# The odd feed-forward block's plain products moved from the end into the first pair of a Strassen-tiled encoder block

## The chip, the cores and the metric

The kernel runs on one core of a Trainium2 chip. The metric is device time in microseconds (us), the median of the runs shown. A core has five engines, each with its own instruction queue that is worked off in order: TensorE (PE, matrix products), VectorE (DVE), ScalarE (ACT), GpSimd (POOL) and SyncE (SP, which here only issues DMAs). Semaphores order them against one another.

## The reference

One layer of a streaming encoder on 256 positions of 2048 channels, in float32: RMS norm, a combined input projection, a gated spatial branch, a sparse-attention branch, an output projection, a residual add; then the part that matters here, a norm and a SwiGLU feed-forward block with 5632 hidden columns, a residual add, and a last norm:

```python
        hn = rms_norm(h, norm2_g[l])
        h = h + (jax.nn.silu(hn @ w_ff_gate[l]) * (hn @ w_ff_up[l])) @ w_ff_down[l]
    return rms_norm(h, final_g)
```

## The kernel before

Every product is made to float32 accuracy from two rounded halves: an operand is split into a high part (ACT, line 74) and the rest (DVE, line 75), and `mm3` (lines 89 to 91) issues three matmuls, high x high, high x low of the weights, low x high. All weights pass through these two splits, so each weight tile costs a load on SP's queue, an ACT copy and a DVE subtraction before PE can use it.

The feed-forward block has 11 column blocks of 512, numbered 0 to 10. Blocks 0 to 9 are done in five pairs, block 10 is the odd one. For a pair, `s_group` makes a gate or an up product over all 16 tiles of the contraction, in eight chunks of 1 MB. Four of them (j = 0 to 3) go by Strassen's scheme: seven products in place of eight, 21 matmuls, but DVE first makes four sums of weight tiles (lines 534 to 536) and both the raw tiles and the sums are split. The other four (j = 4 to 7) are plain: 24 matmuls and one split of 128x2048. The chunks come in the order 0, 4, 1, 5, 2, 3, 6, 7, so Strassen chunks 2 and 3 stand next to each other. `plain_group` is the ordinary product, with chunks of 24 matmuls and one split each; it makes block 10's gate and up products and every down product (`down_one`).

Buffers: 3 for raw weights, 3 each for split halves of 128x2048 (plain chunks and split sums share them), 2 each for those of 128x1536, one for sums. PSUM has four banks "aux" and four "acc"; an `s_group` uses all eight.

Order: PE's order is that of the code, since lines 625 and 626 fix it by hand. Those of ACT, DVE and SP are set by a scheduler at build time, by priorities in code order. The code order before is: pair 0's gate and up groups; pairs 1 to 4, each with gate, two down products of the pair before it, up, the other two; block 10's gate, the transposes of blocks 8 and 9 (`a_operand`, on PE, then split by ACT and DVE), block 10's up; the down products of blocks 8 and 9 (two chunks for each of the four output columns n), among them block 10's down weights are split and kept; at the end the closing section (`last`) multiplies block 10 with the kept weights, adds the residual and makes the last norm, one half of the rows after the other.

Of the kernel before, what the change touches and what calls it, by code (L numbers as in the profile page):

```python
# [12 lines left out]
AF = mybir.ActivationFunctionType  # L13
ALU = mybir.AluOpType
# [5 lines left out]
KT = D // P  # L20
# [9 lines left out]
NFB = FF // 512  # L30
# [10 lines left out]
def block_kernel(ctx: ExitStack, tc: tile.TileContext, a, out):  # L41
# [5 lines left out]
    nc = tc.nc  # L47
# [10 lines left out]
    def t_tile(name, dt=F32R):  # L58
        return tp.tile([P, 4, T], dt, tag="T", name=name)
# [28 lines left out]
    def mm3(o, lh, ll, rh, rl, start, stop, **kw):  # L88
        nc.tensor.matmul(o, lh, rh, start=start, stop=False, **kw)  # L89
        nc.tensor.matmul(o, lh, rl, start=False, stop=False, **kw)  # L90
        nc.tensor.matmul(o, ll, rh, start=False, stop=stop, **kw)  # L91

    def nat_group(w, ks, x, name):


        acc = [acc_tile(f"{name}_{t}") for t in range(2)]
        for c in range(len(ks) // 2):
            wh, wl = wchunk(w[c], 1024)
            for j in range(2):
                i = 2 * c + j  # L100
                xh, xl = x(ks[i])
                for t in range(2):
                    s = slice(t * P, (t + 1) * P)
                    mm3(acc[t], xh[:, s], xl[:, s], wh[:, j * 512:(j + 1) * 512],
                        wl[:, j * 512:(j + 1) * 512], i == 0, i == len(ks) - 1)
        return acc
# [91 lines left out]
    def x_of(k):  # L198
        return xh_t[k // 4][:, k % 4], xl_t[k // 4][:, k % 4]
# [29 lines left out]
    for k in range(KT):  # L229
# [6 lines left out]
        xh, xl = x_of(k)  # L236
        for b in range(2):
            for t in range(2):
                s = slice(t * P, (t + 1) * P)
# [37 lines left out]
    for j in range(2):  # L277
        s = slice(64 * j, 64 * j + 64)
# [148 lines left out]
    for n in range(4):  # L427
        for j in range(2):
            g = 2 * n + j
            s = slice(256 * j, 256 * j + 256)  # L430
# [4 lines left out]
        h, l = t_tile(f"yah{n}"), t_tile(f"yal{n}")  # L435
# [3 lines left out]
    def of(pairs):  # L439
        def f(k):  # L440
            h, l = pairs[k // 4]
            return h[:, k % 4], l[:, k % 4]
        return f
# [10 lines left out]
    for n in range(4):  # L454
        ga = gate(n)
        acc = nat_group(a["w_oa"][n], KS, of(ya), f"oa{n}")
# [3 lines left out]
    for n in range(4):  # L460
        gb = gate(4 + n)
        acc = nat_group(a["w_ob"][n], KS, of(yb), f"ob{n}")
# [3 lines left out]
        h, l = t_tile(f"mxh{n}"), t_tile(f"mxl{n}")  # L466
# [6 lines left out]
    for n in range(4):  # L473
        hx = tp.tile([P, 2, 512], F32, tag="T", name=f"h{n}")
        nc.sync.dma_start(hx, x_nat[n])
        acc = nat_group(a["w_out"][n], KS, of(mx_t), f"out{n}")
        for t in range(2):
            nc.vector.tensor_tensor(hx[:, t], acc[t], hx[:, t], op=ALU.add)
        if 2 * n >= NS:
            h, l = t_tile(f"hh{n}"), t_tile(f"hl{n}")  # L480
# [13 lines left out]
    r2 = row_rstd(ss2, "r2")  # L494
# [6 lines left out]
    def f_tile(name):  # L501
        return fp.tile([P, 2, 512], F32, tag="F", name=name, bufs=3)

    def quad(src):
        raw = wq.tile([P, 4, 512], F32, tag="raw", name="raw")
        nc.sync.dma_start(raw, src)
        return raw

    def quad_split(raw, n=4):
        h, l = (wq.tile([P, n, 512], F32R, tag=f"w{z}{n}", name=f"w{z}", bufs=n - 1 if n < 4 else 3) for z in "hl")  # L510
        split(h, l, raw)
        return h, l
# [61 lines left out]
    def plain_group(chunks, x, n_k, name, bank=acc_tile):  # L574

        acc = [bank(f"{name}_{t}") for t in range(2)]
        for i, c in enumerate(chunks):
            wh, wl = quad_split(quad(c))
            for j in range(4):
                k = 4 * i + j  # L580
                for t in range(2):
                    xh, xl = x(k, t)
                    mm3(acc[t], xh, xl, wh[:, j], wl[:, j], k == 0, k == n_k - 1)
        return acc

    at = {}

    def a_operand(b, s):
        h, l = t_tile(f"ah{b}"), t_tile(f"al{b}")
        transposed(s, f"a{b}", h, l)  # L590
        at[b] = (h, l)

    def gate_blocks(i, beside):
        f, _ = s_group(a["w_fg"][i], f"fg{i}", beside)
        s = [f_tile(f"s{i}_{j}") for j in range(2)]
        for j in range(2):
            for t in range(2):
                f(t, j, s[j][:, t])
                nc.scalar.activation(s[j][:, t], s[j][:, t], AF.Silu, scale=r2[:, t:t + 1])
        return s  # L600

    def up_blocks(i, s):
        f, u = s_group(a["w_fu"][i], f"fu{i}")
        for j in range(2):
            for t in range(2):
                f(t, j)
        for j in range(2):
            nc.vector.tensor_tensor(s[j], s[j], u[:, 2 * j:2 * j + 2], op=ALU.mult)

    def down_one(b, n):  # L610


        acc = plain_group([a["w_fd"][n, b + j] for j in range(2)],
                          lambda k, t: tuple(z[:, k % 4, t * P:(t + 1) * P] for z in at[b + k // 4]),
                          8, f"fd{n}", acc_tile if n % 2 else aux_tile)
        for t in range(2):
            nc.vector.scalar_tensor_tensor(hn[n][:, t], acc[t], r2[:, t:t + 1], hn[n][:, t],
                                           op0=ALU.mult, op1=ALU.add)
# [5 lines left out]

    order = ctx.enter_context(ExitStack())
    order.enter_context(tc.manual_schedule(engines={mybir.EngineType.PE}))
    s = None
    b = NFB - 1
    for i in range(b // 2 + 1):
        done = s  # L630

        def transposes():
            if done is not None:
                for j in range(2):
                    a_operand(2 * i - 2 + j, done[j])
        if i < b // 2:
            s = gate_blocks(i, transposes)
            for n in (0, 1) if i else ():
                down_one(2 * i - 2, n)
            up_blocks(i, s)  # L640
            for n in (2, 3) if i else ():
                down_one(2 * i - 2, n)

    acc = plain_group([a["w_fg10"][c] for c in range(4)], plain_x, KT, f"fg{b}", aux_tile)
    transposes()
    s = f_tile(f"s{b}")
    for t in range(2):
        nc.scalar.activation(s[:, t], acc[t], AF.Silu, scale=r2[:, t:t + 1])
    acc = plain_group([a["w_fu10"][c] for c in range(4)], plain_x, KT, f"fu{b}")
    for t in range(2):  # L650
        nc.vector.tensor_tensor(s[:, t], acc[t], s[:, t], op=ALU.mult)
    kept = []
    for n in range(4):
        down_one(b - 2, n)
        if n < 2:
            raw = quad(a["w_fd"][n, b])
            kept.append([])
            for c in range(2):
                h, l = (tp.tile([P, 2, 512], F32R, tag="T", name=z) for z in ("kept_h", "kept_l"))
                split(h, l, raw[:, 2 * c:2 * c + 2])  # L660
                kept[n] += [(h[:, k], l[:, k]) for k in range(2)]
        if n == 1:
            a_operand(b, s)
    for n in (2, 3):
        h, l = quad_split(quad(a["w_fd"][n, b]))
        kept.append([(h[:, k], l[:, k]) for k in range(4)])
    order.close()

    fg = []
    for i in range(2):  # L670
        f = f_tile(f"fg{i}")
# [1 line left out]
        fg.append(f)  # L673

    o_nat = out.rearrange("(t p) (n c) -> t p n c", p=P, c=512)
    xh, xl = at[NFB - 1]

    def last(t, n, c0, w, ss):
        acc = acc_tile(f"last{n}")[:, :w]
# [9 lines left out]
    for t in range(2):  # L689
# [11 lines left out]
        for n in (2, 0, 3, 1):  # L701
            h = hn[n][:, t]
# [75 lines left out]
```

## Time and the profile before

| | |
|---|---|
| three runs | 1628.66, 1626.4, 1628.76 us, median 1628.66 |
| profiled execution | 1625.63 us, of it 1623.8 us span |
| mean granted TensorE clock | 0.992 of full speed |
| PE busy | 1593.5 us (98%), 7834 matmuls |
| DVE busy | 1098.9 us (68%) |
| ACT busy | 777.9 us (48%) |
| DMA | 307.48 MB, 189 GB/s over the span |

A busy PE isn't PE at its peak: the ends of matmuls are modelled, and a matmul at the halved clock counts as busy for longer. The distance between the starts of two matmuls tells more. In the chain of work that ended last PE has 88% and DVE 7%.

### The profile page before, as it was taken

The numbers are of one execution on the slowest core, as the hardware profiler recorded it, in microseconds if no ns is written. First come the engines' busy times: TensorE is split into PE (matmuls) and PEld (weight loads), VectorE is DVE, ScalarE is ACT, GpSimd is POOL, SyncE is SP. The second block draws the span as 40 slices with busy tenths as digits, with TensorE's granted clock in tenths as the row PEclk, the third lists the DMA queues.
The fourth block names the chain that finished last, engine by engine and source line by source line (L and its number), as shares of the span: only waits on it lengthen the run. The fifth ranks groups of instructions, "written<-read, shape, count | busy, mean of one in ns | idle before, by whom it ended". The sixth has DMA issues, their size and how long they took to land.

```text
span 1623.8 us, 19653 instructions
## 1 busy us (share of the span) xinstructions
PE 1593.5 (98%) x7834; PEld 1340.2 (83%) x7834; DVE 1098.9 (68%) x1208; ACT 777.9 (48%) x815; POOL 1.6 (0%) x8
## 2 busy tenths in 40 slices
PE   9999999999999999999998899999999999999997
PEld 8988989889788888888886777788888888888886
DVE  5695665565754444555565888878888888887565
ACT  6554464555544444444453563644544543554442
POOL 0000000000000000000000000000000000000000
PEclk9999999999999999999999999999999999999999
DMA  9646545555455555555664545555555555545561
GB/s 312 210 140 198 188 162 186 175 171 182 153 169 195 193 193 191 188 187 190 206 208 155 187 176 181 207 200 189 198 201 198 198 190 208 207 183 206 207 233 52
DMA packets 69115, 307.48 MB, mean 189 GB/s; under 512 B 8160, under 2 KB 8416, under 8 KB 52128
## 3 DMA queue, kind: packets, MB, share of 16 engines
q1 hardware_dynamic: 69024, 306.24, 54.9%
q8 instruction: 61, 1.00, 0.3%
q14 instruction: 30, 0.25, 0.0%
HBM read 304.11 MB, written 2.10 MB: 189 GB/s over the span
## 4 chain that ended last, share of the span: by engine, by line
PE 88%; DVE 7%; ACT 2%; issue 1%; DMA 0%; ACTq 0%; SPq 0%; DVEq 0%
PE fd L91 4%; PE fd L90 4%; PE fd L89 4%; DVE wl L75 4%; PE g L91 4%; PE g L90 4%; PE g L89 4%; PE fu_c L91 2%; PE fu_c L90 2%; PE fu_c L89 2%; ACT wh L74 2%; PE q L121 2%; PE q L124 2%; PE q L123 2%; PE u L91 2%; PE u L89 2%
## 5 line engine op out<-in xcount | busy, mean ns | idle before, releaser
L75 DVE TENSOR_TENSOR wl<-raw,wh 128x1024 fp32r<-128x1024 f32 (+3 forms) x434 | 639.5, 1476 | 382.8 <-ACT wh L74 382.1
L74 ACT ACTIVATE wh<-raw 128x1024 fp32r<-128x1024 f32 (+3 forms) x434 | 545.3, 1262 | 549.2 <-PE g L91 86.0
L74 ACT ACTIVATE wh<-sums 128x2048 fp32r<-128x2048 f32 x40 | 76.7, 1917 | 181.1 <-DVE sums L536 153.5
L75 DVE TENSOR_TENSOR wl<-sums,wh 128x2048 fp32r<-128x2048 f32 x40 | 91.7, 2292 | 67.4 <-ACT wh L74 67.4
L89 PE MATMUL fd<-wh,ah 128*128 128x512 f32 x320 | 124.6, 389 | 0.0
L91 PE MATMUL fd<-wh,al 128*128 128x512 f32 x320 | 124.5, 389 | 0.0
L90 PE MATMUL fd<-wl,ah 128*128 128x512 f32 x320 | 124.5, 389 | 0.0
L91 PE MATMUL g<-wh,xl 128*128 128x512 f32 x256 | 100.9, 394 | 0.0
L89 PE MATMUL g<-wh,xh 128*128 128x512 f32 x256 | 100.7, 393 | 0.0
L90 PE MATMUL g<-wl,xh 128*128 128x512 f32 x256 | 99.9, 390 | 0.0
L121 PE MATMUL q<-xh,wh 128*128 128x256 f32 x256 | 72.4, 283 | 0.0
L124 PE MATMUL q<-xh,wl 128*128 128x256 f32 x256 | 72.4, 283 | 0.0
L123 PE MATMUL q<-xl,wh 128*128 128x256 f32 x256 | 72.4, 283 | 0.0
L90 PEld LDWEIGHTS fd<-wl,ah 128*128 128x128 f32 x320 | 60.1, 188 | 12.5
L91 PEld LDWEIGHTS fd<-wh,al 128*128 128x128 f32 x320 | 60.1, 188 | 12.4
L89 PEld LDWEIGHTS fd<-wh,ah 128*128 128x128 f32 x320 | 60.1, 188 | 12.4
L90 PE MATMUL fg_c<-wl,hh 128*128 128x512 f32 x160 | 62.4, 390 | 0.5 <-DVE wl L75 0.5
L89 PE MATMUL fg_c<-wh,hh 128*128 128x512 f32 x160 | 62.6, 391 | 0.0
L91 PE MATMUL fg_c<-wh,hl 128*128 128x512 f32 x160 | 62.3, 389 | 0.0
L89 PE MATMUL fu_c<-wh,hh 128*128 128x512 f32 x160 | 62.2, 389 | 0.0
L90 PE MATMUL fu_c<-wl,hh 128*128 128x512 f32 x160 | 62.2, 389 | 0.0
L91 PE MATMUL fu_c<-wh,hl 128*128 128x512 f32 x160 | 62.2, 389 | 0.0
(303 smaller groups left out, 3423.9 us busy)
## 6 DMA issues: line engine op xcount, KB each, us to landing
raw<-in_w_fg SPq DMA_DIRECT2D x44, 1024.0 KB, 4.8
raw<-in_w_fu SPq DMA_DIRECT2D x44, 1024.0 KB, 4.8
raw<-in_w_fd SPq DMA_DIRECT2D x44, 1024.0 KB, 4.8
raw<-in_w_z SPq DMA_DIRECT2D x64, 512.0 KB, 3.4
raw<-in_w_g SPq DMA_DIRECT2D x64, 512.0 KB, 3.3
raw<-in_w_q SPq DMA_DIRECT2D x32, 512.0 KB, 3.3
raw<-in_w_oa SPq DMA_DIRECT2D x32, 512.0 KB, 3.2
raw<-in_w_ob SPq DMA_DIRECT2D x32, 512.0 KB, 3.3
```

The costliest lines, as they stand in the source:

```text
L74: nc.scalar.activation(h, src, AF.Copy)
L75: nc.vector.tensor_tensor(l, src, hf, op=ALU.subtract)
L89: nc.tensor.matmul(o, lh, rh, start=start, stop=False, **kw)
L90: nc.tensor.matmul(o, lh, rl, start=False, stop=False, **kw)
L91: nc.tensor.matmul(o, ll, rh, start=False, stop=stop, **kw)
L121: nc.tensor.matmul(o, wh[:, s], xh, start=(i == 0 and ct % 2 == 0), stop=False, skip_group_check=True)
L123: nc.tensor.matmul(o, wh[:, s], xl, start=False, stop=False, skip_group_check=True)
L124: nc.tensor.matmul(o, wl[:, s], xh, start=False, stop=last, skip_group_check=True)
```

## The change

Block 10's gate product now comes first in the feed-forward block, its up product between pair 0's gate and up groups, its transposes in the last chunk of pair 0's up group, and its four down products behind that group, one chunk each. Blocks 8 and 9 are transposed between the two last down products of blocks 6 and 7. Block 8's down products stand alone at the end (one chunk for each n), and block 9 is the one whose down weights are kept for the closing section. The gate product of block 10 takes acc banks and its up product aux banks, the other way round than before. The number of matmuls and transposes, the loads and their sizes stay what they were.

```diff
-    def up_blocks(i, s):
-        f, u = s_group(a["w_fu"][i], f"fu{i}")
+    def up_blocks(i, s, beside=None):
+        f, u = s_group(a["w_fu"][i], f"fu{i}", beside)
...
-    def down_one(b, n):
-        acc = plain_group([a["w_fd"][n, b + j] for j in range(2)],
+    def down_one(b, n_b, n):
+        acc = plain_group([a["w_fd"][n, b + j] for j in range(n_b)],
...
-                          8, f"fd{n}", acc_tile if n % 2 else aux_tile)
+                          4 * n_b, f"fd{n}", acc_tile if n % 2 else aux_tile)
...
+    LB = NFB - 1
+
+    def odd_gate():
+        acc = plain_group([a["w_fg10"][c] for c in range(4)], plain_x, KT, f"fg{LB}")
+        s = f_tile(f"s{LB}")
+        for t in range(2):
+            nc.scalar.activation(s[:, t], acc[t], AF.Silu, scale=r2[:, t:t + 1])
+        return s
+
+    def odd_up(s):
+        acc = plain_group([a["w_fu10"][c] for c in range(4)], plain_x, KT, f"fu{LB}", aux_tile)
+        for t in range(2):
+            nc.vector.tensor_tensor(s[:, t], acc[t], s[:, t], op=ALU.mult)
+
+    odd = odd_gate()
+    for i in range(LB // 2):
+        if i == 0:
+            s = gate_blocks(0, None)
+            odd_up(odd)
+            up_blocks(0, s, lambda: a_operand(LB, odd))
+            for n in range(4):
+                down_one(LB, 1, n)
+            continue
...
+        s = gate_blocks(i, transposes)
+        for n in (0, 1):
+            down_one(2 * i - 2, 2, n)
+        up_blocks(i, s)
+        for n in (2, 3):
+            down_one(2 * i - 2, 2, n)
+            if n == 2 and i == LB // 2 - 1:
                 for j in range(2):
-                    a_operand(2 * i - 2 + j, done[j])
-        if i < b // 2:
-            s = gate_blocks(i, transposes)
-            for n in (0, 1) if i else ():
-                down_one(2 * i - 2, n)
-            up_blocks(i, s)
-            for n in (2, 3) if i else ():
-                down_one(2 * i - 2, n)
-
-    acc = plain_group([a["w_fg10"][c] for c in range(4)], plain_x, KT, f"fg{b}", aux_tile)
-    transposes()
-    s = f_tile(f"s{b}")
-    for t in range(2):
-        nc.scalar.activation(s[:, t], acc[t], AF.Silu, scale=r2[:, t:t + 1])
-    acc = plain_group([a["w_fu10"][c] for c in range(4)], plain_x, KT, f"fu{b}")
-    for t in range(2):
-        nc.vector.tensor_tensor(s[:, t], acc[t], s[:, t], op=ALU.mult)
+                    a_operand(2 * i + j, s[j])
+
     kept = []
     for n in range(4):
-        down_one(b - 2, n)
+        down_one(LB - 2, 1, n)
         if n < 2:
-            raw = quad(a["w_fd"][n, b])
+            raw = quad(a["w_fd"][n, LB - 1])
...
-        if n == 1:
-            a_operand(b, s)
...
-    xh, xl = at[NFB - 1]
+    xh, xl = at[LB - 1]
```

Three places show how the queues of DVE and ACT are moved by it. The names: `wl<-raw` is the split of raw weights (128x2048 a plain chunk, 128x1536 a Strassen chunk), `sums` the Strassen sums, `wl<-sums` their split, `h_...<-fd` the eviction of a down product, `r_` the row norm, `s_` the blocks' hidden values.

DVE at the start of the feed-forward block, before:

```order
L534 TENSOR_TENSOR sums<-raw 128x1024
L143 TENSOR_SCALAR r_r<-r_y 128x2
L535 TENSOR_TENSOR sums<-sums,raw 128x512
L75 TENSOR_TENSOR wl<-raw,wh 128x1536
L536 TENSOR_TENSOR sums<-sums,raw 128x512
L75 TENSOR_TENSOR wl<-sums,wh 128x2048
```

And DVE there now:

```order
L143 TENSOR_SCALAR r_r<-r_y 128x2
L75 TENSOR_TENSOR wl<-raw,wh 128x2048 x4
L534 TENSOR_TENSOR sums<-raw 128x1024
L75 TENSOR_TENSOR wl<-raw,wh 128x1536
L535 TENSOR_TENSOR sums<-sums,raw 128x512
L536 TENSOR_TENSOR sums<-sums,raw 128x512
L75 TENSOR_TENSOR wl<-sums,wh 128x2048
```

Four plain splits now stand ahead of the first Strassen sums, and the first split of weights comes with no sum ahead of it.

DVE from the end of pair 0's up group to the first chunks of pair 1's gate group, before:

```order
L608 TENSOR_TENSOR s_0_7845<-s_0_7845,fu_u 128x1024
L608 TENSOR_TENSOR s_1_7846<-s_1_7846,fu_u 128x1024
L75 TENSOR_TENSOR wl<-raw,wh 128x2048
L534 TENSOR_TENSOR sums<-raw 128x1024
L75 TENSOR_TENSOR wl<-raw,wh 128x1536
```

And DVE there now:

```order
L608 TENSOR_TENSOR s_1_7971<-s_1_7971,fu_u 128x1024
L75 TENSOR_TENSOR wl<-raw,wh 128x2048
L617 SCALAR_TENSOR_TENSOR h_6825<-fd_0_8400,r_r,h_6825 128x512
L617 SCALAR_TENSOR_TENSOR h_6825<-fd_1_8401,r_r,h_6825 128x512
L75 TENSOR_TENSOR wl<-raw,wh 128x2048
L534 TENSOR_TENSOR sums<-raw 128x1024
L617 SCALAR_TENSOR_TENSOR h_7009<-fd_0_8434,r_r,h_7009 128x512
L617 SCALAR_TENSOR_TENSOR h_7009<-fd_1_8435,r_r,h_7009 128x512
L535 TENSOR_TENSOR sums<-sums,raw 128x512
L75 TENSOR_TENSOR wl<-raw,wh 128x1536
L536 TENSOR_TENSOR sums<-sums,raw 128x512
```

The evictions of block 10's four down products, two for each, now stand between the preparation of pair 1's first Strassen chunks; each waits for PE.

ACT at the end of the program, from the first banks of the last up group on, before:

```order
L549 ACTIVATE fu_u<-fu_m_11135 128x512
L74 ACTIVATE wh<-raw 128x2048 x10
L648 ACTIVATE s_11697<-fg_0_11543,r_r 128x512
L648 ACTIVATE s_11697<-fg_1_11544,r_r 128x512
L74 ACTIVATE ah_11665<-a_pt_11667 128x512
```

And ACT there now:

```order
L549 ACTIVATE fu_u<-fu_m_11536 128x512
L74 ACTIVATE wh<-raw 128x2048 x5
L74 ACTIVATE ah_11880<-a_pt_11882 128x512
L74 ACTIVATE ah_11880<-a_pt_11889 128x512
L74 ACTIVATE ah_11896<-a_pt_11898 128x512
L74 ACTIVATE ah_11896<-a_pt_11905 128x512
L74 ACTIVATE kept_h<-raw 128x1024 x2
```

The transposes of blocks 8 and 9 come five splits after those banks instead of ten, with the kept weights right behind them.

## Rows read from the trace of the kernel before

**Rows 1.** PE's waits: who waited for whom, total us, times, longest us.

```profile
PE fg_m L90 <- DVE wl L75: 10.9, 9, 3.2
```

**Rows 2.** Timeline of PE, first chunks of the feed-forward block: start, us, instruction, [idle before].

```profile
887.89 0.80 PE L89 MATMUL fg_m<-wh,hS_h 128*128 128x512 f32 x1 [3.26 <-ACT wh L74]
891.88 0.80 PE L90 MATMUL fg_m<-wl,hS_h 128*128 128x512 f32 x1 [3.19 <-DVE wl L75]
...
896.75 0.79 PE L90 MATMUL fg_m<-wl,hS_h 128*128 128x512 f32 x1 [1.53 <-DVE wl L75]
...
900.33 0.50 PE L89 MATMUL fg_c<-wh,hS_h 128*128 128x512 f32 x1
...
900.89 0.39 PE L91 MATMUL fg_c<-wh,hS_l 128*128 128x512 f32 x1
...
902.50 0.39 PE L89 MATMUL fg_c<-wh,hh 128*128 128x512 f32 x1
...
907.94 0.39 PE L89 MATMUL fg_m<-wh,hS_h 128*128 128x512 f32 x1
...
912.70 0.39 PE L89 MATMUL fg_c<-wh,hh 128*128 128x512 f32 x1
```

**Rows 3.** Timeline of PE, the rest of pair 0 and pair 1's gate.

```profile
940.09 0.39 PE L89 MATMUL fu_m<-wh,hS_h 128*128 128x512 f32 x1
...
944.66 0.60 PE L90 MATMUL fu_m<-wl,hS_h 128*128 128x512 f32 x1 [3.50 <-DVE wl L75]
...
986.28 0.39 PE L89 MATMUL fg_m<-wh,hS_h 128*128 128x512 f32 x1
...
1012.54 0.50 PE L90 MATMUL fg_m<-wl,hS_h 128*128 128x512 f32 x1 [1.66 <-DVE wl L75]
...
1019.61 0.50 PE L90 MATMUL fg_m<-wl,hS_h 128*128 128x512 f32 x1 [1.82 <-DVE wl L75]
...
1032.01 1.91 PE L152 MATMUL a_pt<-ident,s 128*128 128x128 f32 x16
1036.49 0.39 PE L89 MATMUL fd<-wh,ah 128*128 128x512 f32 x1
```

**Rows 4.** Instruction groups from 880 to 1040 us: busy us, mean ns | idle before.

```profile
L75 DVE TENSOR_TENSOR wl<-sums,wh 128x2048 fp32r<-128x2048 f32 x12 | 27.5, 2291 | 19.0 <-ACT wh L74 19.0
...
L74 ACT ACTIVATE wh<-sums 128x2048 fp32r<-128x2048 f32 x12 | 23.0, 1916 | 55.3 <-DVE sums L536 55.3
...
L534 DVE TENSOR_TENSOR sums<-raw 128x1024 f32<-128x1024 f32 x12 | 14.6, 1219 | 0.1
...
L536 DVE TENSOR_TENSOR sums<-sums,raw 128x512 f32<-128x512 f32 x12 | 8.2, 687 | 0.2
```

**Rows 5.** Timelines of DVE (four rows) and ACT (two): start, us, instruction.

```profile
890.08 1.75 DVE L75 TENSOR_TENSOR wl<-raw,wh 128x1536 fp32r<-128x1536 f32 x1
...
896.61 2.28 DVE L75 TENSOR_TENSOR wl<-raw,wh 128x2048 fp32r<-128x2048 f32 x1
...
987.30 2.35 DVE L608 TENSOR_TENSOR s<-s,fu_u 128x1024 f32<-128x1024 f32 x2
...
1491.81 1.43 DVE L617 SCALAR_TENSOR_TENSOR h<-fd,r_r,h 128x512 f32<-128x512 f32 x2 [0.52 <-PE fd L91]
...
886.37 1.47 ACT L74 ACTIVATE wh<-raw 128x1536 fp32r<-128x1536 f32 x1
...
940.36 1.28 ACT L599 ACT_TABLE_LOAD   x1
```

**Rows 6.** Windows: us, busy PE, PEld, DVE, ACT, POOL, PE's clock, DMA share, GB/s.

```profile
986.00:1027.00 41.00, 36.34 (x148) 28.45 (x148) 33.47 (x27) 16.31 (x10) 0.00 (x0) 0.96 0.45 157
...
1130.00:1150.00 20.00, 19.75 (x88) 16.03 (x87) 15.62 (x12) 9.06 (x6) 0.00 (x0) 1.00 0.46 158
...
1506.00:1550.00 44.00, 44.00 (x204) 36.69 (x203) 23.87 (x16) 19.89 (x16) 0.00 (x0) 1.00 0.64 226
```

**Rows 7.** The page's part 6: loads of down weights, number, KB, us to landing.

```profile
raw<-in_w_fd SPq DMA_DIRECT2D x44, 1024.0 KB, 4.8
```

More of the change, by code (lines that the diff above doesn't have):

```diff
@@ L626, in block_kernel @@
     order.enter_context(tc.manual_schedule(engines={mybir.EngineType.PE}))
-    s = None
-    b = NFB - 1
-    for i in range(b // 2 + 1):
+    LB = NFB - 1
[9 more added lines that the diff above has]
+            nc.vector.tensor_tensor(s[:, t], acc[t], s[:, t], op=ALU.mult)
@@ L630, in block_kernel @@
+    odd = odd_gate()
[7 more added lines that the diff above has]
+            continue
         done = s
         def transposes():
-            if done is not None:
-                for j in range(2):
-                    a_operand(2 * i - 2 + j, done[j])
-        if i < b // 2:
-            s = gate_blocks(i, transposes)
-            for n in (0, 1) if i else ():
-                down_one(2 * i - 2, n)
-            up_blocks(i, s)
-            for n in (2, 3) if i else ():
-                down_one(2 * i - 2, n)
@@ L644, in block_kernel @@
-    acc = plain_group([a["w_fg10"][c] for c in range(4)], plain_x, KT, f"fg{b}", aux_tile)
-    transposes()
-    s = f_tile(f"s{b}")
-    for t in range(2):
-        nc.scalar.activation(s[:, t], acc[t], AF.Silu, scale=r2[:, t:t + 1])
-    acc = plain_group([a["w_fu10"][c] for c in range(4)], plain_x, KT, f"fu{b}")
-    for t in range(2):
-        nc.vector.tensor_tensor(s[:, t], acc[t], s[:, t], op=ALU.mult)
+            for j in range(2):
+                a_operand(2 * i - 2 + j, done[j])
+        s = gate_blocks(i, transposes)
@@ L661, in block_kernel @@
                 kept[n] += [(h[:, k], l[:, k]) for k in range(2)]
-        if n == 1:
-            a_operand(b, s)
     for n in (2, 3):
-        h, l = quad_split(quad(a["w_fd"][n, b]))
+        h, l = quad_split(quad(a["w_fd"][n, LB - 1]))
         kept.append([(h[:, k], l[:, k]) for k in range(4)])
```

## The prediction

> **What bounds the kernel now.** I read PE's waits first, since a kernel whose matmuls fill nearly the whole span can only gain where PE stands still. The largest entry is PE waiting for DVE's weight splits in the gate groups' Strassen products, nine times, 10.9 us together [rows 1]. The timeline of PE says where: nearly all of it lies in three groups, pair 0's gate and up and pair 1's gate [rows 2, 3]. A wait costs more than its idle time, because behind some of them the clock falls to its lower level, 1.2 in place of 2.4 GHz: starts lie 0.43 us apart in place of 0.23 [rows 2], so I count lost time from starts, not from idle columns. A plain chunk needs 907.94 − 902.50 = 5.44 us for 24 matmuls, a Strassen chunk 912.70 − 907.94 = 4.76 us for 21 [rows 2], 0.227 us each, and a group of four and four 40.8 us. What the groups took instead:
>
> - Pair 0's gate: PE idles 3.26 us before its first product, and then takes 940.09 − 887.89 = 52.2 us, 11.4 too many [rows 2, 3]. Of these, 9.8 go in the first 14 matmuls (900.89 − 887.89 = 13.0 us for 3.2 us of work).
> - Pair 0's up: 986.28 − 940.09 = 46.2 us, 5.4 too many, from one wait of 3.50 us and the slow clock behind it [rows 3].
> - Pair 1's gate: 1036.49 − 986.28 = 50.2 us, less 1.7 us for 16 transposes (they are recorded as 1.91, but their starts take that much less): 48.5, so 7.7 too many, with waits of 1.66 and 1.82 us [rows 3].
>
> Together 27.8 us. The later pairs are nearly free of it: the stretch with pair 2's first wait has PE busy for 19.75 of 20 us [rows 6], and with the slower restart I count 0.6 us for each of pairs 2 to 4. The end is full: 44.00 of 44 us, DVE at 23.87 [rows 6].
>
> The cause is DVE's work per chunk. A Strassen chunk costs it one sum of 1.2 us, two of 0.7, a split of 1.75 and one of 2.3, some 6.6 us [rows 4, 5], against 4.76 us on PE; a plain chunk costs 2.3 against 5.44. A Strassen group is 36 us of DVE plus some 5 us of evictions, about PE's 40.8. Three such groups in a row leave DVE no slack to catch up; in the worst of them it is busy for 33.47 of 41 us even with all the waiting [rows 6]. Later pairs have four plain down chunks ahead of each group, 3 us of DVE slack in every one.
>
> **The change, part by part.** No matmul, transpose, load or split is added or removed, so the sum is made of waits alone.
>
> *Start.* The first weights to be split are now a plain chunk. ACT starts at 886.37 as before, but copies 2048 columns in place of 1536: about 1.9 us (as the sums' copy of that width [rows 4]) in place of 1.47 [rows 5], so the first matmul comes near 888.35, after 3.7 us idle. DVE then has no sum ahead of the split. Before, the second product had to wait for two sums and the split, until 891.88; now for 2.28 us [rows 5] from about 888.45, when the norm's last small step is done, until 890.75. That is 2.2 us lost behind the first product. From there the second and third split (one each 2.2 us) stay ahead of chunks of 5.44 us, so PE runs through; the clock is slow at first, as from 896.75 to 900.33, nine starts in 3.6 us [rows 2], 1.6 too many, say 1.8 with the step back. Sum 3.7 + 2.2 + 1.8 = 7.7 us, against 3.26 + 9.8 = 13.1 before: 5.4 saved. Bounds for the 7.7: 5.9 if the clock stays up, 10.7 if all 24 matmuls run slowly.
>
> *Rest of pair 0's gate.* It starts 21.8 us after the first chunk, and DVE has 9.2 us of splits in that time, so by walking the queue the first Strassen chunk is ready some 4 us early, and the tightest place, chunk 3's sums behind chunk 2's, 2 us early. Saved: 11.4 − 9.8 = 1.6 us (0 to 1.6). Two new waits stand in the queues. ACT's Silu of block 10 waits for the last odd gate product, and behind it the copy of chunk 1's sums; but PE wants those 12 us later (4.76 + 5.44 + the chunk's first 2 us), and table load, two Silus, copy and split take about 7. The fifth product of the gate group waits for a bank that this Silu frees, 2.7 us after it became due. Both at nothing.
>
> The Trainium skill speaks against such an order: "TensorE: Matmul & The Clock Gate", section "Architectural detail", says that ScalarE and VectorE are strict FIFOs, so whatever stands behind the Silu is held with it. By that rule the price is the 5 us of cover turning into a wait only if the Silu came 5 us late; It leaves the sum at 17.2.
>
> *Pair 0's up.* It now follows four plain chunks, and by the same walk its first sums are split before it starts. The 5.4 us fall to what the bank change costs: the up group's third product takes an aux bank that DVE's two multiplications of block 10 free, about 1.4 us (as the pair of evictions, 1.43 [rows 5]) after the odd up product ends, while the two first products take 1.4. I take 0.2 (0 to 1.4). Saved 5.2.
>
> *Pair 1's gate.* It follows four one-chunk down products, 21.8 us on PE. DVE owes in that time: evictions of the up group and two multiplications (four 512-wide steps like L536's 0.69, start to start 0.6 [rows 4], and 2.35 [rows 5], together 4.8 us), four down splits (two of them early), eight evictions at 0.7, and the first chunks of the gate. Counted from the start of the down products, with each eviction waiting for its product (10.9, 16.3, 21.8 us): first Strassen chunk ready at 21.7, when PE wants it; first plain split 23.9; last two evictions 25.3; chunk 1 at 32.3; second plain 34.5; chunk 2 at 44.5, wanted at 44.4; chunk 3, by 2.7 us of sums, 1.95 of ACT and 2.3 of split [rows 4], at 51.4, wanted at 49.2. So one wait of 2.2 us, 2.5 with its restart, against 7.7 before: 5.2 saved. Bounds: 0.6, where it is like pairs 2 to 4, and 7.7, unchanged.
>
> The clock may fall behind that wait. In the trace it stays up after 1.66 us at 1012.54 and falls after the 1.82 us that follow at 1019.61, and after 3.50 at 944.66 [rows 3], so 2.2 lies between. I take it as staying up; falling costs 1.8 more.
>
> The Trainium skill, same page, section "What's actually happening", has the monitor's window run freely, so that how much runs slowly depends on where in it the work lands. By that both outcomes can occur from run to run; with the fall the sum would be 15.4 in place of 17.2.
>
> *Pairs 1 to 4 otherwise.* Same chunks, same neighbours: 0.
>
> *End.* Before, the products of block 10 stood between the last up group and blocks 8 and 9's transposes. Now the last up group is followed by one down product of two chunks (10.9 us), and PE transposes after it. The hidden values need 5 us of DVE behind the group, so they are ready; one of the four banks is that of the down product just ended, whose two evictions take 1.43 us against 0.9 us of transposes to other banks: 0.2 us (0 to 1.5). The splits of these transposes stand on ACT behind one weight copy, with 10.9 us of down product to hide them. In SP's queue the last norm's gain waits for block 8's transposes, with five loads behind it; each of these needs a buffer freed later than that, and lands 4.8 us after issue [rows 7], so nothing. DVE's work from the end of the last up group to the closing section: evictions and multiplications 4.8, splits 8 × 2.2, kept halves 4 × 1.1, 12 evictions at 0.7, four small splits 2.4, together some 38 of 45 us. It fits, but with 7 us to spare where before it was half idle.
>
> Sum: 5.4 + 1.6 + 5.2 + 5.2 − 0.2 = 17.2 us. The profiled execution's 1625.63 (its span is 1.8 shorter) goes to 1608.4. The three runs lie at 1626.4 to 1628.76 with the median 3 us above the profiled one; taken from the median, 1628.66 − 17.2 = 1611.5.
>
> **The rivals.** *Pair 1's gate stays short of DVE:* the eight evictions, each waiting for PE in DVE's queue, take back what the four down chunks give, and its 7.7 us stay. For it: my walk has no slack there, and DVE's queue has those evictions between the sums. Against it: 21.8 us of plain products hold 9 us of splits. Gain 12.0, 1616.7; with the start at its worse bound 9.0, 1619.7.
>
> *Slower, by the end of the program:* DVE goes into the last 45 us with a backlog and PE waits for the splits of the kept weights. From 7 us of backlog on each further us costs one; it is slower than before from 7 + 17 = 24 us, eleven splits. At 30 us: 1628.7 + 6 = 1634.5. Against it: three buffers of a kind let no such backlog stand, and before the change DVE waited for ACT there.
>
> *No change:* DVE, not PE, sets the time of the first two pairs, and the waits only move behind the moved products. Time 1628.7. Against it: three groups ask some 122 us of DVE and as much of PE (three times 40.8); with twelve plain chunks among them it is 122 + 12 × 2.2 + 8 × 0.7, about 154, for 122 + 12 × 5.44 = 187 on PE.
>
> *Better:* start and pair 1's gate at their good bounds, gain 20.9: 1607.8.
>
> **How the numbers follow.** Forecast, 1608.7 to 1615: 0.60. Pair 1's gate short, 1615 to 1620: 0.25. Better than 1608.7: 0.07. No change: 0.04. Slower: 0.04. The range takes the forecast, its neighbour and 2.5 us of the better side, with 1 us for the spread of the medians: 1606 to 1620. A measurement of this kernel tells 0.2%, 3.3 us, from no change: faster 0.92, same 0.04, slower 0.04.
>
> **What would show it.** Start: first matmul half a us later than 887.89, second near 890.7, no wait then for 40 us. Pair 0: no wait over 0.5 us in gate or up. Pair 1's gate: one wait near 2 us at chunk 3; two or more, or the slow clock, mean the first rival. End: the 16 transposes in one piece, PE full until the closing section, 44 of 44 us. It would be wrong if new waits stood behind the Silu on ACT or behind block 10's multiplications on DVE.

## The result, and the profile after

| | before | after |
|---|---|---|
| median, executions of the first comparison | 1627.53 us (4) | 1608.03 us (4) |
| ratio, 95% interval | | 0.9891 [0.9879, 0.9902] |
| profiled execution, of it span | 1625.63, 1623.8 us | 1608.13, 1606.3 us |
| mean granted TensorE clock | 0.992 | 0.996 |
| PE busy, matmuls | 1593.5 us, 7834 | 1587.4 us, 7834 |
| DVE busy | 1098.9 us | 1103.8 us |

The kernel became 1.1% faster. The two profiled executions differ by 17.5 us; the forecast was 17.2.

In the chain of work that ended last DVE had 7%. After the change it reads (shares of the span by engine):

```profile
PE 93%; DVE 4%; ACT 2%; issue 0%; DMA 0%; SPq 0%; ACTq 0%; DVEq 0%
```

PE's waits after, to be held against [rows 1] (who waited for whom, total us, times, longest us):

```profile
PE fg L89 <- ACT wh L74: 3.7, 1, 3.7
PE fg_m L90 <- DVE wl L75: 2.3, 4, 1.6
PE fg L90 <- DVE wl L75: 1.6, 1, 1.6
```

The large entry fell from 10.9 us in nine waits to 2.3 in four, and the up group's entry of 3.5 us is gone. The two others are the waits of the first chunk, which is now a plain one; before, PE waited there for ACT and DVE at a Strassen chunk, 3.26 and 3.19 us and more [rows 2].

The timeline of PE from the first chunk on, which answers [rows 2, 3]:

```profile
888.61 0.79 PE L89 MATMUL fg<-wh,hS_h 128*128 128x512 f32 x1 [3.69 <-ACT wh L74]
891.05 0.79 PE L90 MATMUL fg<-wl,hS_h 128*128 128x512 f32 x1 [1.65 <-DVE wl L75]
...
895.05 0.47 PE L90 MATMUL fg<-wl,hS_h 128*128 128x512 f32 x1
895.37 0.40 PE L91 MATMUL fg<-wh,hS_l 128*128 128x512 f32 x1
...
914.67 0.39 PE L89 MATMUL fg_m<-wh,hS_h 128*128 128x512 f32 x1
...
955.47 0.39 PE L89 MATMUL fu<-wh,hS_h 128*128 128x512 f32 x1
...
977.23 0.39 PE L89 MATMUL fu_m<-wh,hS_h 128*128 128x512 f32 x1
...
1018.93 0.39 PE L89 MATMUL fd<-wh,ah 128*128 128x512 f32 x1
...
1040.69 0.39 PE L89 MATMUL fg_m<-wh,hS_h 128*128 128x512 f32 x1
...
1069.87 0.50 PE L90 MATMUL fg_m<-wl,hS_h 128*128 128x512 f32 x1 [1.59 <-DVE wl L75]
...
1080.66 1.91 PE L152 MATMUL a_pt<-ident,s 128*128 128x128 f32 x16
...
1085.14 0.39 PE L89 MATMUL fd<-wh,ah 128*128 128x512 f32 x1
```

The distances between these starts are the result. The odd gate takes 26.06 us, 4.30 more than its 96 matmuls need at 0.227 us. Pair 0's gate takes 955.47 − 914.67 = 40.80 and the odd up product 21.76, nothing too many. Pair 0's up takes 1018.93 − 977.23 = 41.70, which is 40.8 and 0.9 for eight transposes; the four down products take 21.76. Pair 1's gate takes 1085.14 − 1040.69 = 44.45; less 1.7 for its transposes and 40.8 that leaves 1.9 too many, from one wait of 1.59 us.

ACT's and DVE's first splits after, for [rows 5] (three of 128x2048 in a piece):

```profile
886.66 5.50 ACT L74 ACTIVATE wh<-raw 128x2048 fp32r<-128x2048 f32 x3
```

```profile
888.71 6.70 DVE L75 TENSOR_TENSOR wl<-raw,wh 128x2048 fp32r<-128x2048 f32 x3
```

Windows after, for [rows 6] (busy PE, PEld, DVE, ACT, POOL, clock, DMA share, GB/s):

```profile
986.00:1027.00 41.00, 41.00 (x187) 34.04 (x186) 32.26 (x28) 19.68 (x13) 0.00 (x0) 1.00 0.53 184
...
1506.00:1550.00 44.00, 44.00 (x204) 36.65 (x204) 34.00 (x30) 21.19 (x16) 0.00 (x0) 1.00 0.58 203
...
1530.00:1575.00 45.00, 45.00 (x209) 37.49 (x208) 35.87 (x32) 21.08 (x16) 0.00 (x0) 1.00 0.56 198
```

PE is full in the stretch of [rows 6] that had the slow clock, and it is still full at the end, where DVE now works for 34.00 of 44 us instead of 23.87. The means of [rows 4] (here from 880 to 1100 us) and the time to landing of [rows 7] stayed nearly what they were:

```profile
L75 DVE TENSOR_TENSOR wl<-sums,wh 128x2048 fp32r<-128x2048 f32 x13 | 29.8, 2292 | 20.9 <-ACT wh L74 20.9
```

```profile
raw<-in_w_fd SPq DMA_DIRECT2D x44, 1024.0 KB, 4.7
```

### The profile page after: what moved, and what is told of

Its sections match the earlier page's. It is cut to its first block, busy times and chain, and to the rows that moved or that the text cites. A ratio compares the mean times of both kernels' runs of the same rounds, so it can differ in the third digit from the quotient of the medians.

```text
span 1606.3 us, 19668 instructions
## 1 busy us (share of the span) xinstructions
PE 1587.4 (99%) x7834; PEld 1337.8 (83%) x7834; DVE 1103.8 (69%) x1216; ACT 778.1 (48%) x815; POOL 1.6 (0%) x8
## 4 chain that ended last, share of the span: by engine, by line
PE 93%; DVE 4%; ACT 2%; issue 0%; DMA 0%; SPq 0%; ACTq 0%; DVEq 0%
PE fd L90 4%; PE fd L89 4%; PE fd L91 4%; PE g L89 4%; PE g L91 4%; PE g L90 4%; PE fu_c L90 3%; PE fu_c L91 3%; PE fu_c L89 3%; DVE wl L75 2%; PE fg_c L91 2%; PE fg_c L89 2%; PE fg_c L90 2%; PE q L124 2%; PE q L121 2%; PE q L123 2%
## 5 line engine op out<-in xcount | busy, mean ns | idle before, releaser
L89 PEld LDWEIGHTS fd<-wh,ah 128*128 128x128 f32 x320 | 60.1, 188 | 12.5
L91 PEld LDWEIGHTS fd<-wh,al 128*128 128x128 f32 x320 | 60.1, 188 | 12.5
```

## The experiments

The question is which of the moved parts brought what, whether it was DVE's backlog that they paid for, and what is left. Everything is counted as in the prediction: us lost by PE, from starts, against 0.227 us a matmul. "Start" is PE's idle time ahead of the first chunk and what is lost in that chunk.

| us lost | start | rest of pair 0's gate | pair 0's up | pair 1's gate | three later gates | end |
|---|---|---|---|---|---|---|
| before | 13.1 | 1.6 | 5.4 | 7.7 | 1.7 | 0 |
| e1b: gate first | 8.6 | 0 | 2.6 | 9.0 | 1.6 | 0 |
| e2b: gate and up | 8.3 | 0 | 0 | 4.5 | 1.7 | 0 |
| after: gate, up and down | 8.0 | 0 | 0 | 1.9 | 1.7 | 0 |
| e5: after, no evictions | 8.2 | 0 | 0 | 0 | 1.6 | 0 |
| e7: after, other order | 8.2 | 0 | 0 | 0 | 0 | 0 |
| e9: before, other order | 13.5 | 0 | 6.6 | 9.7 | 0 | 0 |
| e3: before, no sums | 8.4 | 0 | 0 | 0 | 0 | 0 |

A few tenths in the first column mean nothing: the changed kernel itself lost 8.0 us there in its first trace and 7.7 in its second (c_after).

### One part at a time: the gate product first

```diff
+    acc = plain_group([a["w_fg10"][c] for c in range(4)], plain_x, KT, f"fg{b}")
+    odd = fp.tile([P, 2, 512], F32, tag="odd", name=f"s{b}")
...
-    acc = plain_group([a["w_fg10"][c] for c in range(4)], plain_x, KT, f"fg{b}", aux_tile)
-    transposes()
```

> The kernel before with one part of the change alone: block 10's gate product (and its Silu) stands first in the feed-forward block; its up product, its transposes and its down products stay at the end. The pool of hidden values has two buffers and one apart for block 10, in the same space. Theory (each group of pair 0 and pair 1 loses its time for want of plain products ahead of it): the start falls from 13.1 to 7.7 us and the rest of pair 0's gate from 1.6 to 0, while pair 0's up keeps its 5.4 us and pair 1's gate its 7.7. Saved 7.0 us, about 1620.5. Rival (a head start once given is kept by DVE through the three groups): up and pair 1's gate lose clearly less too, saved 12 us or more. Rival (the gain came from the shorter end of the program): no gain here.

It came to 1624.01 us, 0.9979 [0.997, 0.9989]. That is 3.5 us more than the theory's 1620.5. The start lost 8.4 us, near the 7.7 expected, but this kernel had made a wait of its own: without the gate product ahead of them, nothing on PE covered the splits of blocks 8 and 9's transposes. PE's timeline at the end:

```profile
1545.23 0.50 PE L89 MATMUL fd<-wh,ah 128*128 128x512 f32 x1 [3.19 <-DVE al L75]
```

With the slow restart that is 5.1 us. So the same part was tried again with the transposes ahead of block 10's up product.

> Only block 10's gate product goes first, as in e1_gate_first, but the transposes of blocks 8 and 9 stand ahead of block 10's up product, so that it covers their splits. Theory: e1's loss at the end (one wait of 3.19 us and the slow clock behind it, 4.9 us by starts) was of that experiment's own making and goes; what remains is 9.0 us at the start, 2.6 in pair 0's up and 8.8 in pair 1's gate, so about 1619 to 1619.5. Rival, that moving the odd products away from the end costs something there by itself: the loss at the end stays, 1623 to 1624.

It came to 1617.74 us, 0.9948 [0.9935, 0.996], 1.3 us below the theory's 1619, and the loss at the end was gone. Two of the groups behind still wait; PE's timeline in pair 0's up and pair 1's gate:

```profile
985.86 0.50 PE L90 MATMUL fu_m<-wl,hS_h 128*128 128x512 f32 x1 [1.82 <-DVE wl L75]
...
1006.20 0.80 PE L90 MATMUL fg_m<-wl,hS_h 128*128 128x512 f32 x1 [5.77 <-DVE wl L75]
```

Pair 0's up lost 2.6 us in place of 5.4, though no plain product stands in front of it here, and pair 1's gate 9.0 in place of 7.7. So the odd gate's head start reaches over one group into the next, and part of what is saved there is only put off to the one after.

### Two parts: gate and up products

```diff
             s = gate_blocks(i, transposes)
+            if i == 0:
+                acc = plain_group([a["w_fu10"][c] for c in range(4)], plain_x, KT, f"fu{b}", aux_tile)
+                for t in range(2):
+                    nc.vector.tensor_tensor(odd[:, t], acc[t], odd[:, t], op=ALU.mult)
```

> As the run before, and also block 10's up product between pair 0's gate and up groups; its transposes and down products stay at the end. Theory: pair 0's up loses its 5.4 us as well, pair 1's gate keeps its 7.7. Saved 7.0 + 5.2 = 12.2 us, about 1615.3. The difference to the full change, about 5.2 us, is then what the four down products ahead of pair 1's gate are worth. Rival (head start is kept): pair 1's gate is already near 2 us here, and the full change adds nothing.

1615.63 us, 0.9933 [0.9919, 0.9948], with the same 3.19 us at the end, and 4.5 us lost in pair 1's gate. The size was met by two errors: the gate lost less than expected, the end more. Again without the end's wait:

> Block 10's gate and up products stand where the changed kernel has them, its down products stay at the end, and the transposes of blocks 8 and 9 stand between two down products of blocks 6 and 7, as in the changed kernel. Theory: the loss of e2_gate_up at the end goes (4.9 us), what it lost in pair 1's gate (4.5 us against 1.9 in the changed kernel) stays: about 1610.7. So the four down products ahead of pair 1's gate are worth 2.6 us, half of the 5.2 that the prediction gave them, and the other half is the up product's. Rival, that the down products are worth their 5.2 us: about 1613.

1611.72 us, 0.9911 [0.9897, 0.9924]. That is 1 us more than the theory's and 1.3 less than the rival's, and medians alone would leave it open; the trace decides. Pair 1's gate has these two waits and loses 4.5 us, as forecast:

```profile
1033.44 0.50 PE L90 MATMUL fg_m<-wl,hS_h 128*128 128x512 f32 x1 [1.39 <-DVE wl L75]
...
1051.18 0.50 PE L90 MATMUL fg_m<-wl,hS_h 128*128 128x512 f32 x1 [1.82 <-DVE wl L75]
```

Of what else the profiled execution (1612.10 us) has over the changed kernel's, 1.1 us lies ahead of the feed-forward block, where the kernels are alike: the last transposes there begin at 884.48 us in this execution and at 883.37 in that of the changed kernel. So, added in this order, the up product is worth 2.6 us in pair 0's up and 4.5 in pair 1's gate, and the four down products 2.6.

### The suspected cause taken away: no sums

The kernel before, with the low and high halves of the raw tile in the places of the Strassen sums (the sums are left out, the matmuls stay):

```diff
-                nc.vector.tensor_tensor(tt[:, 0:2], raw[:, 1:3], raw[:, 0:1].to_broadcast([P, 2, 512]), op=ALU.add)
-                nc.vector.tensor_tensor(tt[:, 2], tt[:, 0], raw[:, 2], op=ALU.add)
-                nc.vector.tensor_tensor(tt[:, 3], tt[:, 2], raw[:, 3], op=ALU.add)
...
-                th, tl = quad_split(tt)
+                th, tl = quad_split(raw)
```

> The kernel before, its order untouched, but the three sums that DVE makes for each Strassen chunk are left out: the raw tiles are split a second time in their place, so the output is not the reference's. DVE then has 2.65 us less for each of 40 chunks. Theory (PE's waits in the first three groups are DVE's throughput): the waits in pair 0's up and pair 1's gate are gone (5.4 + 7.7 + 1.6 us), the start falls from 13.1 to about 7, pairs 2 to 4 lose their 0.6 each. Saved about 22 us, near 1606, with nothing moved. Rival (the waits come from buffers, loads or ACT's copies): under 8 us saved, with waits of 1 us and more left in pair 0's up and pair 1's gate.

1605.58 us, 0.9872 [0.9857, 0.9887]. PE's waits in the feed-forward block, all within the first chunk:

```profile
PE fg_m L89 <- ACT wh L74: 3.3, 1, 3.3
PE fg_m L90 <- DVE wl L75: 2.4, 2, 1.8
```

With about 2.6 us less of DVE work in each Strassen chunk every later wait is gone, without a product being moved. DVE's time per Strassen chunk was the cause. That time is not all work, though. In the kernel before, the split of the sums stands right behind them in DVE's queue and waits there for ACT's copy: 19.0 us of idle ahead of twelve such splits [rows 4]. The edit took away these waits with the sums, so it doesn't tell how much of the loss was DVE's work and how much its waiting; a kernel with the sums in which other splits fill these gaps wasn't run.

### What is left in pair 1's gate: the evictions or the order

DVE's timeline in the changed kernel, from the split of chunk 2's sums to that of chunk 3's:

```profile
1060.45 2.29 DVE L75 TENSOR_TENSOR wl<-sums,wh 128x2048 fp32r<-128x2048 f32 x1 [2.04 <-ACT wh L74]
1062.78 1.23 DVE L534 TENSOR_TENSOR sums<-raw 128x1024 f32<-128x1024 f32 x1
1064.04 0.69 DVE L535 TENSOR_TENSOR sums<-sums,raw 128x512 f32<-128x512 f32 x1
1064.76 0.69 DVE L536 TENSOR_TENSOR sums<-sums,raw 128x512 f32<-128x512 f32 x1
1067.52 2.29 DVE L75 TENSOR_TENSOR wl<-sums,wh 128x2048 fp32r<-128x2048 f32 x1 [2.07 <-ACT wh L74]
```

There is one buffer of sums, so chunk 3's begin when chunk 2's are split: three sums, ACT's copy while DVE waits 2.07 us, the split; 7.07 us from one split to the next, where PE spends 4.76 on a chunk. Chunk 2's were ready at 1062.74 and PE wanted them at about 1063.4; chunk 3 can't be in time then. The eight evictions were left out first:

```diff
-        for t in range(2):
+        for t in range(2) if b != NFB - 1 else ():
             nc.vector.scalar_tensor_tensor(hn[n][:, t], acc[t], r2[:, t:t + 1], hn[n][:, t],
```

> The changed kernel, with the eight evictions of block 10's down products left out (the products are made, but not added to the residual, so the output lacks block 10's share). In the changed kernel pair 1's gate still loses 1.9 us, nearly all of it in one wait of 1.59 us for DVE's split at chunk 3. Theory: those eight evictions, which stand between the sums and splits of pair 1's first Strassen chunks on DVE and cost about 0.7 us each, make that wait; without them it falls to the 0.25 us of the later pairs, and the profiled execution gets about 1.5 us shorter (1606.6 against 1608.1). Rival: the wait comes from the order sums, copy, split of chunks 2 and 3, which stand next to each other, and from the single buffer of the sums; then it stays at 1.6 us and the time at 1608.1.

1607.24 us, 0.9882 [0.9867, 0.9897]. The median moved by 0.8 us only, but in the trace the wait went altogether, not to 0.25 us. The window of pair 1's gate, and DVE's timeline:

```profile
1041.00:1085.00 44.00, 44.00 (x204) 36.65 (x204) 34.60 (x29) 20.59 (x16) 0.00 (x0) 1.00 0.58 204
```

```profile
1056.49 2.29 DVE L75 TENSOR_TENSOR wl<-sums,wh 128x2048 fp32r<-128x2048 f32 x1 [2.07 <-ACT wh L74]
...
1065.11 2.29 DVE L75 TENSOR_TENSOR wl<-sums,wh 128x2048 fp32r<-128x2048 f32 x1 [2.06 <-ACT wh L74]
```

Chunk 2's split comes 4 us earlier, though the group itself starts 1.5 us later (at 1042.18), and the distance of the two splits, now 8.6 us, doesn't matter any more. The time of the profiled execution (1607.65 us) hides it, because that execution entered the feed-forward block late, at 884.66 instead of 883.37. The evictions make the wait; but the other theory isn't excluded by that, since a chunk between 2 and 3 could make it harmless just as well:

```diff
-    ORDER = (0, 4, 1, 5, 2, 3, 6, 7)
+    ORDER = (0, 4, 1, 5, 2, 6, 3, 7)
```

> The changed kernel with the chunks of an s_group in the order 0, 4, 1, 5, 2, 6, 3, 7, so that a plain chunk stands between Strassen chunks 2 and 3. Leaving out the evictions has already taken away the wait in pair 1's gate; this leaves them in and moves the chunk that waits 5.44 us later. Theory: what the changed kernel still loses in its Strassen groups (1.9 us in pair 1's gate, 0.55 in each later gate) comes of DVE's 6.6 us for each of two Strassen chunks in a row against PE's 4.76; all of it goes, 3.5 us, to about 1604.5. Rival: the evictions push the whole queue of DVE back, and the wait moves to chunk 2 or 1 with its size: 1608.

1605.32 us, 0.9865 [0.9852, 0.9879], beside the changed kernel itself:

> The changed kernel once more, beside the three that follow on the same chip: 1608.0, with the one wait of 1.6 us at chunk 3 of pair 1's gate.

1608.03, as before. The other order saves 2.7 us by medians, and all 3.6 us that were left in the Strassen groups; the start lost 0.4 more in the profiled execution (8.2 us against 7.7 in c_after), which also began the block 0.9 us later. The same window of pair 1's gate, with DVE working for more than in e5:

```profile
1041.00:1085.00 44.00, 44.00 (x204) 36.68 (x203) 37.60 (x32) 20.86 (x16) 0.00 (x0) 1.00 0.59 203
```

So both are conditions of that wait, and either one taken away removes it.

### Would the order alone have done it?

> The kernel before with nothing changed but the chunk order, 0, 4, 1, 5, 2, 6, 3, 7. Theory: its losses in pair 0's up and pair 1's gate are a backlog of DVE carried from group to group (three groups ask about as much of DVE as of PE), which another order inside the groups does not pay back: over half of the 13 us stays, and the start's 13.8 with it, so 1619 or more. Rival: it is the two Strassen chunks side by side alone; then the 13 us and the 1.6 of pair 0's gate go, 1611 to 1612, and the moved block was not needed for more than the start.

1627.51 us, 1.0004 [0.9995, 1.0012]: nothing. PE's timeline of the two groups:

```profile
941.94 0.50 PE L90 MATMUL fu_m<-wl,hS_h 128*128 128x512 f32 x1 [2.22 <-DVE wl L75]
...
991.60 0.79 PE L90 MATMUL fg_m<-wl,hS_h 128*128 128x512 f32 x1 [4.49 <-DVE wl L75]
...
1035.72 0.66 PE L152 MATMUL a_pt<-ident,s 128*128 128x128 f32 x4 [1.50 <-DVE fg_u L553]
```

The order takes away the 1.6 us of pair 0's gate and the 1.7 of the later ones, and the table shows where they went: 1.2 into pair 0's up and 2.0 into pair 1's gate with its transposes, which now wait for DVE too (the 0.4 more at the start is no more than two traces of one kernel differ there). In a stretch that DVE sets, a better order moves waits; only once the plain products pay the backlog does it remove them, as in e7.

### How much room DVE has at the end

```diff
+        if i == LB // 2 - 1:
+            extra = fp.tile([P, 4, 512], F32, tag="u", name="extra")
+            for _ in range(10):
+                tc.keep_in_program_order(nc.vector.tensor_tensor(extra[:, 0:2], hn[0], hn[0], op=ALU.add))
```

> The changed kernel with ten more additions of 128x1024 on DVE, whose results nobody reads, spread over the last 45 us: some 11.4 us of DVE work, where the windows of the changed kernel show DVE busy for about 70% of that stretch. The prediction's rule was that from 7 us of backlog at the end each further us costs one: 11.4 - 7 = 4.4 us lost, 1612.4 to 1612.5 for the median. Rival: DVE's idle time at the end takes the additions up, PE finds its splits in time, and less than 0.5 us is lost (1608.0 to 1608.5).

1612.14 us, 0.9913 [0.99, 0.9927]; by starts 3.6 us lost. The size is near the rule's 4.4, so the rival falls, but the place isn't the one the rule gives. The window from 1533 to 1565 us has DVE busy for nearly all of it, against 26.31 us in the changed kernel:

```profile
1533.00:1565.00 32.00, 30.47 (x141) 24.78 (x140) 31.62 (x29) 13.13 (x12) 0.00 (x0) 1.00 0.50 177
```

PE's waits there, and DVE's timeline at the first two:

```profile
1542.14 0.66 PE L152 MATMUL a_pt<-ident,s 128*128 128x128 f32 x4 [0.39 <-DVE h L617]
1543.93 0.66 PE L152 MATMUL a_pt<-ident,s 128*128 128x128 f32 x4 [1.14 <-DVE h L617]
...
1567.88 0.50 PE L90 MATMUL fd<-wl,ah 128*128 128x512 f32 x1 [1.02 <-DVE wl L75]
```

```profile
1540.21 1.22 DVE L664 TENSOR_TENSOR extra<-h 128x1024 f32<-128x1024 f32 x1
1541.34 0.74 DVE L617 SCALAR_TENSOR_TENSOR h<-fd,r_r,h 128x512 f32<-128x512 f32 x1
1542.01 1.21 DVE L664 TENSOR_TENSOR extra<-h 128x1024 f32<-128x1024 f32 x1
1543.14 0.74 DVE L617 SCALAR_TENSOR_TENSOR h<-fd,r_r,h 128x512 f32<-128x512 f32 x1
```

Half of the loss, 2.0 us, is two evictions that stand behind two additions while PE's transposes wait for the banks that they free; the rest is mostly the split of a weight chunk that came 1.02 us late, with its restart. It is a matter of who stands where in the queue before it is one of the sum. The Trainium skill ("TensorE: Matmul & The Clock Gate", section "Architectural detail") calls VectorE's queue a strict FIFO; these rows agree, 1.14 us for an eviction that was due and stood behind an addition.

### The start, and both together

The start is the largest loss left, 8.0 us. PE needn't stand still there: the odd gate's first three chunks take the first twelve of the sixteen tiles of the normed input, and these exist before the output product's last quarter is done. The changed kernel, with those chunks split during that quarter (short form):

```diff
+    ws3 = [quad_split(quad(a["w_fg10"][c])) for c in range(3)]
+    for t in range(2):
+        tc.keep_in_program_order(nc.vector.tensor_tensor(hx[:, t], acc[t], hx[:, t], op=ALU.add))
...
+    for i in range(2):
+        odd_chunk(i, *ws3[i])
+    h, l = t_tile("hh3"), t_tile("hl3")
+    transposed(hx, "h3", h, l, scale=g2[:, 12:16])
+    odd_chunk(2, *ws3[2])
...
+    odd_chunk(3, *quad_split(quad(a["w_fg10"][3])))
```

> The changed kernel with its start rearranged: the first three weight chunks of block 10's gate are split while the last output product still runs (ACT and DVE idle some 8 us there), PE goes from that product straight into the first two chunks, and the last block's residual add, transposes, their split, the sums of squares and the row norm come beside them. Same work. Theory (what is left at the start, 7.7 us and 0.7 at the transposes, is only the order of ACT's and DVE's queues behind the last output product): PE no longer waits there and its clock does not fall, 8 us saved against the changed kernel, about 1600. Rival (the buffers or the loads of these weights are not free earlier): the splits wait all the same, under 2 us saved, about 1607.

1600.33 us, 0.984 [0.9824, 0.9857]. PE goes from the output product into the odd gate without a gap:

```profile
882.29 0.39 PE L91 MATMUL out<-wh,mxl 128*128 128x512 f32 x1
882.52 0.39 PE L89 MATMUL fg<-wh,hS_h 128*128 128x512 f32 x1
```

With the other order on top:

> The kernel of e4_start_early (the odd gate's first chunks split during the output product) with the chunk order 0, 4, 1, 5, 2, 6, 3, 7. Theory: both savings stand beside each other, since one lies at the start and one in the Strassen groups: 1600.3 - 3.4, about 1597. Rival: the new order costs something where the last products of a group are combined, with one plain chunk instead of two to cover it: 1600 or more.

1596.19 us, 0.9811 [0.9798, 0.9824] of the kernel before, and 11.8 us less than the changed kernel beside it. PE's largest wait in the whole feed-forward block, and the chain of work that ended last:

```profile
PE fg_c L89 <- ACT s L665: 0.4, 1, 0.4
```

```profile
PE 98%; DVE 1%; ACT 0%; DMA 0%; issue 0%; SPq 0%; ACTq 0%
```

From 882 us to the closing section PE loses 0.7 us by starts, against 12.5 in the changed kernel and 30 before. The two savings stand beside each other. Only fewer or faster matmuls would bring more here.

## Why the prediction was right, and where its terms were off

Its steps against the rows:

- **Start**, 5.1 us saved against 5.4. The first matmul waits 3.69 us (3.7) and the second comes 2.44 later (2.2 lost, as forecast). The slow clock behind it lasts until 895.05, 2.1 us against the 1.8 that were put down. That is within the spread of the term: in nine profiled executions with this first chunk it cost between 1.5 (e2) and 2.7 us (e1b), and 1.8 in c_after, the same kernel. (The nine starts from which the term was taken are eight distances, 1.8 us too many and not 1.6.)
- **Rest of pair 0's gate**, 1.6 saved, as forecast. The Silu and the banks cost nothing here; the wait behind the Silu that the prediction put at nothing shows in e4 and e8 alone, with 0.4 us.
- **Pair 0's up**, 5.4 saved against 5.2: the bank change, taken at 0.2, cost nothing.
- **Pair 1's gate**, 5.8 saved against 5.2. One wait, at chunk 3, 1.59 us against 2.2, and the clock stayed up. For a wait of 2.2 us the rows spoke against that: 2.2 doesn't lie between a wait after which the clock stayed up and one after which it fell, since it had fallen after 1.82 [rows 3], and with the fall the sum was 15.4. That the wait came out shorter was luck for this choice. From 1018.93, where the down products start, chunk 2's sums were split after 43.8 us (walk: 44.5) and chunk 3's after 50.9 (51.4), wanted at 49.2. A walk along DVE's queue with durations of before was good to 0.7 us over 50.
- **End**, 0 against −0.2; DVE worked for 35.87 of the last 45 us, the prediction had 38.

By starts the sum is 5.1 + 1.6 + 5.4 + 5.8 = 17.9 us, of which the part ahead of the block took back 0.3 (its last transposes began at 883.37 instead of 883.08 us): the 17.5 measured, within rounding. The profiled time was forecast at 1608.4 and is 1608.13. So close a hit is in part luck, as the terms were off by −0.3, 0, 0.2, 0.6 and 0.2 us and the part ahead by −0.3. The median was forecast at 1611.5 and is 1608.03, within the range but 3.5 us off: the 1628.66 from which 17.2 was taken is high, since later comparisons with 9 to 15 executions of the kernel before give 1626.1 to 1626.9. A forecast on the median should have started nearer the profiled time. (In the rival of a slow end, 1628.7 + 6 stands as 1634.5; unrounded it is 1628.7 + 5.8.)

The cause that the prediction named was right, but too narrow. It set DVE's work, 36 us a group and 5 of evictions, against PE's 40.8; that comes out even, and would not cost PE 5 to 8 us a group. What it left out there is the 19.0 us for which DVE stood ahead of twelve splits of sums [rows 4], 1.6 us a chunk and some 6 a group. With them a group takes some 47 us of DVE's queue (an estimate from [rows 4, 5]). The walk had this wait, as 1.95 us of ACT, and so the forecast came out.

What the sum didn't show is that its terms aren't separate. The prediction gave each group's gain to the plain products ahead of it: 5.2 us of pair 0's up to the odd up product, 5.2 of pair 1's gate to the four down products. The experiments give the odd gate 2.8 us of the first, and then −1.3 of the second; the up product 2.6 and 4.5; the down products 2.6. These numbers read as if DVE's head start were one store, filled by every plain chunk and emptied by every Strassen chunk, so that where a product stands decides only whether the store is empty too early; no run measured the store by itself. The total was right because the walk was made with all three moved; a forecast for one of them alone by the same terms failed (e1b's pair 0 up and pair 1 gate, and e2b's pair 1 gate, which the term had at 7.7 without the down products and which lost 4.5).

The first rival, pair 1's gate at 7.7 us, wasn't met: the gate lost 1.9 us, and 4.5 even without the down products (e2b). Its mechanism was there on a smaller scale, since the evictions make the wait that was left (e5). The rival of a slow end had its spare 7 us about right in size; that such a backlog first delays an eviction that holds a bank, it had not seen.

## What to carry to other kernels

Where PE waits for another engine's preparation, add up that engine's work, the waits that stand in its own queue, and PE's work over the whole run of groups, not for each: light chunks ahead pay for heavy ones a group or two later, and reordering inside a stretch that the other engine sets only moves the waits. Put the light work first, where the queue is empty, and once the sum is paid for, put a light chunk between any two heavy ones that share a buffer. At the beginning of a stage, start what already has its inputs: the 8 us that e4 got back were lost to a stage boundary that the data didn't ask for.

## What was not expected of the hardware

Waits of the same length left the clock up in one kernel and not in another. PE waited 1.82 us at 1019.61 in the kernel before [rows 3] and at 1051.18 in e2b. The windows around the two, with the granted clock third from the end:

```profile
1018.00:1026.00 8.00, 6.39 (x21) 5.12 (x22) 6.72 (x5) 5.23 (x3) 0.00 (x0) 0.79 0.56 203
```

```profile
1048.00:1056.00 8.00, 6.17 (x27) 4.67 (x26) 7.17 (x4) 6.81 (x5) 0.00 (x0) 1.00 0.48 169
```

In the first the clock fell to the lower level, 1.2 GHz, and starts lie 0.43 us apart for some 3 us; in the second, as behind e1b's 1.82 us at 985.86, it stayed at 2.4. What PE did before differs: in the first case another wait, of 1.66 us, lay 7 us back; in e2b one of 1.39 us lay 18 us back. The Trainium skill ("TensorE: Matmul & The Clock Gate", section "What's actually happening") has the monitor's window run freely, by which the same wait can go either way; the rows agree with that, but don't tell it apart from the earlier wait's share. More for it is that the slow stretch behind one and the same first wait of 3.69 us differs: nine profiled executions show 5 (e2) to 11 (e1b) starts 0.43 us apart.

The times of the kernel before differ in the same way. In the comparisons with the experiments its 37 executions took 1623.8 to 1629.0 us. The six under 1625.4 had a mean granted clock of 0.992 to 0.995, the eight over 1628 one of 0.990 or 0.991. The eight executions of the changed kernel lie within 2.1 us, at 0.996 or 0.997. So a kernel with fewer waits also had the steadier time here.

The part ahead of the feed-forward block, the same in all kernels but e4 and e8, ended up to 1.6 us apart in the profiled executions (883.08 to 884.66 us). Differences of 1 us between two medians of this kernel are therefore read from the stage's own starts or not at all.
